# Group norm's reciprocal root by a table root and one Newton step, and the scratch half of the output projection's squares

## The chip, the cores and the metric

The kernel runs on one core of one Trainium2 chip. TensorE (PE) does the matmuls and its transposes, VectorE (DVE) the elementwise work and reductions, ScalarE (ACT) the copies and functions from a table, GpSimd (POOL) masks and some subtractions, and SyncE (SP) issues nearly all transfers. Each engine works through its own queue in order, and semaphores tie the queues together. The metric is the device time of one execution in microseconds; lower is better.

## The reference

Two layers over 512 positions of width 1024, in float32. Layer 0 mixes tokens by an RWKV-7 recurrence, layer 1 by a spatial gating unit; a gated feed-forward network follows each, and each sub-layer has a norm ahead and a norm behind it. What matters here is the end of the recurrence: its output is normalised per head of 64 values, gets a bonus term, is gated and projected, and the projection's result is normalised over its 1024 columns and added to the input.

```python
def _rmsnorm(x, g):
    x32 = x.astype(jnp.float32)
    y = x32 * lax.rsqrt(jnp.mean(x32 * x32, axis=-1, keepdims=True) + RMS_EPS)
    return (y * g.astype(jnp.float32)).astype(x.dtype)
...
    mu = jnp.mean(y, axis=-1, keepdims=True)
    var = jnp.mean(jnp.square(y - mu), axis=-1, keepdims=True)
    y = (y - mu) * lax.rsqrt(var + GN_EPS)
    y = y * gn_w.reshape(H, N).astype(f32) + gn_b.reshape(H, N).astype(f32)
    y = y + jnp.sum(r_h * k_h * r_k.astype(f32), axis=-1, keepdims=True) * v_h
    y = y.reshape(B, T, D).astype(x.dtype)
    return (y * g) @ w_o
...
        x = x + _rmsnorm(h, norm_gains[i, 1])
```

## The kernel before, in words

Nothing is kept back between stages but on-chip tiles and a few scratch tensors in memory. The 512 positions are four blocks (`tt`) of 128 partitions; the 1024 columns are two halves of 512 or eight groups of 128. Float32 products are made of three matmuls each (`mm3`, line 201) from a high and a low part, which `split` (line 178) makes with one copy on ACT and one subtraction on DVE; `weight` (line 182) loads a weight and splits it.

The recurrence treats the 16 heads in four groups `b` of four. For each group the list `PLAN` (line 35) names the parts in order: P (projections), E (`early`, line 754, with the functions Tanh, Exp and Ln on ACT), X and V (the values' projection), F (`front`, line 838), B (`back`, line 887), S (`scan`, line 985) and N (`finish`, line 1091). `front` builds the chunk matrices; ACT copies them out of the accumulators (the BX copies of lines 873, 883 and 884 among them) and POOL masks them. `back` inverts a triangular matrix: a stream transpose (line 896), a long substitution on DVE (lines 910 and 912), transposes (915 and 916), then small matmuls whose results DVE and ACT copy to `bdT` (lines 949, 959 and 968), and the products `mp` (line 973) and `gh` (line 980), which DVE adds into MV (lines 982 and 983). `scan` steps through eight chunks with the state `su` (lines 1011 and 1014) and copies its output Y out (line 1024).

N is the group norm (line 1031) with what follows it. In `group_norm` DVE sums Y (line 1038) and subtracts the mean (1040), ACT squares (1042), DVE sums the squares into `va` (1044), `rsqrt` (line 209) makes the reciprocal root, and DVE scales Y by it (1046). `rsqrt` works on DVE alone: a scaled sum (line 214), a first guess by an integer shift and subtraction (216 and 218), and three Newton steps of three instructions (221 to 223). It is called on 16 values per partition for the groups 0 to 2 and, for group 3, twice on 8 values: halves of the positions, the first when the scan is half done (line 1130). The text calls these five norms N0, N1, N2 and the first and second half of N3. `rsqrt` is also called four times on one value in the gating unit (line 1205).

`gated` (line 1076) then transposes Y on PE (`yt`, 1084), adds weight and bonus on DVE (1085), makes the gate by matmuls (`gate`, 1087 and 1088) and multiplies (1089). `yt` and `gate` share one accumulator bank, tag `pf`. For groups 0 to 2 the result goes through memory, for group 3 it stays in `OB`.

`out_proj` (line 273) is the output projection, called four times: after the recurrence, after the gating unit and after each feed-forward network. Only the first call passes `spare`. It accumulates eight banks, four blocks by two halves; with `spare` the last weight unit of both halves is held to the end (line 281) and the loop of line 335 finishes block by block. Per block and half, `post0` (line 304) and `post1` (line 314) square the accumulator on ACT with a row sum (`sumsq`, line 235, writing the squares to a scratch tile), DVE multiplies by the gain (lines 309 and 317), and `part` (line 240) and `rsqrt1` (line 248) make the row's reciprocal root: the table root on ACT (254), then reciprocal and one Newton step on DVE (256 to 258). Line 320 adds the result to `x`. The scratch tile `hn` has 1024 columns: `post1` puts its squares into the first half (`lo`) and line 317 writes the second (`hi`). Line 312 is a root on one column whose result nobody reads; it stands at the first block with `spare`, else at the last.

A table set must be on ACT before a function of it can run; where another set is there, the program holds an `ACT_TABLE_LOAD` ahead of the instruction. The order of every queue is laid down before the run by a planner that simulates the program's time (line 1289), starting from the order of the code; it threads instructions of different parts into one another.

Of the kernel before, what the change touches and what calls it, by code (L numbers as in the profile page):

```python
# [7 lines left out]
F32 = mybir.dt.float32  # L8
F32R = mybir.dt.float32r
I32 = mybir.dt.int32  # L10
AF = mybir.ActivationFunctionType
ALU = mybir.AluOpType

P = 128
# [3 lines left out]
TT = T // P  # L18
# [6 lines left out]
GN_EPS = 64e-5  # L25
# [105 lines left out]
class Trunk:  # L131
# [77 lines left out]
    def rsqrt(self, ss, n, scale, eps):  # L209
# [13 lines left out]
            v.scalar_tensor_tensor(y, t, 1.5, y, op0=ALU.add, op1=ALU.mult)  # L223
        return y

    def bcast_row(self, row):

        t = self.gp.tile([P, D], F32, name="gain", tag="gain", bufs=2)
        self.nc.gpsimd.dma_start(out=t, in_=row.partition_broadcast(P))
        return t  # L230
# [42 lines left out]
    def out_proj(self, acts, wrows, nk, row, xts, store=None, tail=3, norm=None, spare=None, mid=None, after=()):  # L273


        nc = self.nc
        v = nc.vector
        gain = self.bcast_row(row)
        nu = nk // 2
        cols = [slice(0, 512), slice(512, 1024)]  # L280
        late = (1, 1) if spare else (0, tail)
        accs, f0, part = [None, None], [], []

        def mms(half, k, tt, w):
            tok = slice(tt * P, (tt + 1) * P)
            hi, lo = acts(k)
            self.mm3(accs[half][tt], (hi[:, tok], lo[:, tok]), w, k == 0, k == nk - 1)

        def unit(half, u):
            own = spare if half and u < nu - late[1] else None  # L290
            with ExitStack() as order:
                for ins in after:
                    order.enter_context(self.tc.issue_after(ins.ins))
                hi, lo = self.weight(wrows(u)[:, :, cols[half]], spare=own)
            return [(2 * u + j, (hi[:, j, :], lo[:, j, :])) for j in range(2)]

        def first(half):
            accs[half] = self.accs(half)
            for u in range(nu - late[half]):
                for k, w in unit(half, u):  # L300
                    for tt in range(TT):
                        mms(half, k, tt, w)

        def post0(tt, junk):
            acc = accs[0][tt]
            s = self.sumsq(acc, junk)
            if tt % 2 == 0:
                f0.append(self.f0p.tile([P, 2, 512], F32, name="f0", tag="f0", bufs=2))
            v.tensor_tensor(f0[-1][:, tt % 2, :], acc, gain[:, cols[0]], op=ALU.mult)
            part.append(self.part(s, 1.0 / D, RMS_EPS))  # L310
            if tt == (0 if spare else TT - 1):
                nc.scalar.activation(junk[:, 0:1], part[tt][0], AF.Sqrt)

        def post1(tt, hn):
            acc, lo, hi = accs[1][tt], hn[:, 0:512], hn[:, 512:1024]
            s = self.sumsq(acc, lo)
            v.tensor_tensor(hi, acc, gain[:, cols[1]], op=ALU.mult)
            y = self.rsqrt1(s, part[tt], 1.0 / D)
            for f, c in ((f0[tt // 2][:, tt % 2, :], cols[0]), (hi, cols[1])):
                v.scalar_tensor_tensor(xts[tt][:, c], f, y[:, 0:1], xts[tt][:, c], op0=ALU.mult, op1=ALU.add)  # L320
                if store is not None and tt == TT - 1:
                    nc.sync.dma_start(out=store[tt * P:(tt + 1) * P, c], in_=xts[tt][:, c])
            if store is not None and tt < TT - 1:
                nc.sync.dma_start(out=store[tt * P:(tt + 1) * P, :], in_=xts[tt])

        hn_tile = lambda: self.sm.tile([P, D], F32, name="hn", tag="hn", bufs=2)
        first(0)
        if not spare:
            for tt in range(TT):
                post0(tt, hn_tile()[:, 0:512])  # L330
        if mid:
            mid()
        first(1)
        ends = [[kw for u in range(nu - late[half], nu) for kw in unit(half, u)] for half in range(2)]
        for tt in range(TT):
            for half in range(2):
                for k, w in ends[half]:
                    mms(half, k, tt, w)
            if norm and tt >= LAG:
                norm.step(tt - LAG, xts[tt - LAG])  # L340
            hn = hn_tile()
            if spare:
                post0(tt, hn[:, 512:1024])
            post1(tt, hn)
        if norm:
            for tt in range(TT - LAG, TT):
                norm.step(tt, xts[tt])
            norm.finish()
# [181 lines left out]
    def rwkv(self, x0):  # L530
        nc, i, tc = self.nc, self.i, self.tc
        v, a, g = nc.vector, nc.scalar, nc.gpsimd
        mm = nc.tensor.matmul
        with ExitStack() as ctx:
# [14 lines left out]
            def e2(name, shape=(P, 2, T), dt=F32):  # L549
                return rp.tile(list(shape), dt, name=name, tag="e2", bufs=E2)  # L550
# [41 lines left out]
            for tt in range(TT):  # L592
                hn = e2("hn", (P, D))
# [437 lines left out]
            def group_norm(Y, tts):  # L1031

                n, n4 = len(tts), 4 * len(tts)
                ts = slice(tts[0], tts[-1] + 1)
                y4 = Y[:, ts].rearrange("p t q (h v) -> p (t q h) v", h=2)
                yf = Y[:, ts].rearrange("p t q f -> p (t q f)")
                mu = self.sm.tile([P, n4], F32, name="mu", tag="mu", bufs=2)
                v.tensor_reduce(mu, y4, axis=mybir.AxisListType.X, op=ALU.add)
                v.tensor_scalar(mu, mu, 1.0 / 64, None, op0=ALU.mult)
                v.tensor_tensor(y4, y4, mu.unsqueeze(2).broadcast_to([P, n4, C]), op=ALU.subtract)  # L1040
                sq = self.sm.tile([P, n4, C], F32, name="hn", tag="hn", bufs=2)
                a.activation(sq.rearrange("p q v -> p (q v)"), yf, AF.Square)
                va = self.sm.tile([P, n4], F32, name="va", tag="va", bufs=2)
                v.tensor_reduce(va, sq, axis=mybir.AxisListType.X, op=ALU.add)
                rs = self.rsqrt(va, n4, 1.0 / 64, GN_EPS)
                v.tensor_tensor(y4, y4, rs.unsqueeze(2).broadcast_to([P, n4, C]), op=ALU.mult)

            def bonus(b, o):
# [42 lines left out]
            def finish(b, o, Y):  # L1091

                tts = (0, 1, 2, 3)
                group_norm(Y, tts)
                w = gate_weights(b)
                for q, ob in enumerate(bonus(b, o)):
                    gated(b, Y, q, ob, w, tts)
                    nc.sync.dma_start(out=od[2 * b + q], in_=ob)
# [3 lines left out]
            def finish_half(b, o, Y, tts):  # L1102
                group_norm(Y, tts)
                for q, ob in enumerate(OB):
                    gated(b, Y, q, ob, GW[0], tts)
# [187 lines left out]
```

## Time and profile before

| what | value |
|---|---|
| median of 3 runs | 1354.4 us (1348.42 to 1357.36) |
| the profiled execution | 1345.89 us |
| its span, first to last instruction | 1344.2 us |
| its mean granted TensorE clock | 0.979 |
| instructions | 24525 |
| group norms | 278 to 437 us of the span |
| first output projection's block loop | about 441 to 470 us |

In the profile's rows a group of instructions has its line, engine, operation, output and inputs, shapes and count, then busy time and the mean in nanoseconds of one, then the idle time just before them and what ended it. In the timeline the columns are start, duration, engine, line, operation, operands, count, and in brackets the idle time before it with the releaser. In the table of stretches each has its length, busy time of PE, weight loads, DVE, ACT and POOL with counts, granted clock, DMA share and GB/s.

### The profile page before, as it was taken

The page shows a single profiled execution, that of the slowest core. Times are in us where ns is not written, and L with a number is a line of the kernel's source. Part 1 is how long each engine was busy: PE and PEld are TensorE (multiplying, and loading weights), DVE is VectorE, ACT ScalarE, POOL GpSimd, SP SyncE. Part 2 cuts the span into 40 slices and gives each one's busy share as a digit, 9 for nine tenths or more (in the row PEclk, how much of TensorE's full clock was granted, in tenths as well). Part 3 has the DMA queues.
Part 4 walks back from the last instruction along what each step waited for, and adds up shares of the span by engine and source line. Part 5 has one row for each costly group of instructions (what it writes and reads, how often), then busy time and mean ns, then how long its engine had stood idle before and what let it go on. Part 6 is the DMA issues. An engine that isn't in the chain of part 4 may idle for free.

```text
span 1344.2 us, 24525 instructions
## 1 busy us (share of the span) xinstructions
PE 1279.7 (95%) x9812; PEld 1115.3 (83%) x9812; DVE 898.5 (67%) x1520; ACT 694.9 (52%) x1240; POOL 166.3 (12%) x306
## 2 busy tenths in 40 slices
PE   5999999988989799999999999999999999999997
PEld 3677799887767698899998887878888999998886
DVE  7975846667856589778775325575689878785223
ACT  7976884757443554445454314543464455464221
POOL 0000373665000121000000002020002000000000
PEclk9999999989889999999999999999999999999999
DMA  5146683412143233333323332343430443323231
GB/s 159 47 107 169 165 199 127 123 47 78 45 139 106 72 91 101 107 114 108 106 87 110 94 112 91 93 140 98 142 95 2 125 126 95 97 78 125 94 94 63
DMA packets 217266, 140.10 MB, mean 104 GB/s; under 512 B 67856, under 2 KB 193344, under 8 KB 217152
## 3 DMA queue, kind: packets, MB, share of 16 engines
q1 hardware_dynamic: 215856, 133.81, 34.6%
q0 software_dynamic: 1296, 4.72, 1.0%
q8 instruction: 77, 1.26, 0.4%
q14 instruction: 37, 0.30, 0.1%
HBM read 124.35 MB, written 14.16 MB: 103 GB/s over the span
## 4 chain that ended last, share of the span: by engine, by line
PE 58%; DVE 5%; ACT 1%; issue 1%; DMA 0%; SPq 0%; DVEq 0%; ACTq 0%
PE acc L204 24%; PE Q L204 11%; PE Z L204 7%; PE R L204 7%; PE gu L204 5%; PE u L204 3%; DVE wlo L180 1%; DVE wsum L387 1%; PE s L1227 1%; PE ptr L267 0%; ACT whi L179 0%; DVE braw L106 0%; DVE hT L62 0%; DVE bc L180 0%; DVE x L320 0%
## 5 line engine op out<-in xcount | busy, mean ns | idle before, releaser
L180 DVE TENSOR_TENSOR wlo<-wraw,whi 128x1024 fp32r<-128x1024 f32 x109 | 133.6, 1226 | 197.8 <-ACT whi L179 197.4
L179 ACT CAST whi<-wraw 128x1024 fp32r<-128x1024 f32 x109 | 114.2, 1048 | 224.1 <-PE acc L204 140.9
L204 PE MATMUL acc<-whi,actw 128*128 128x512 f32 x704 | 220.7, 394 | 0.0
L204 PE MATMUL Q<-bc,whi 128*128 128x256 f32 x864 | 157.2, 282 | 3.5 <-ACT hn L431 2.2
L204 PEld LDWEIGHTS acc<-whi,actw 128*128 128x128 f32 x704 | 132.3, 188 | 30.7
L204 PE MATMUL acc<-wlo,actw 128*128 128x512 f32 x352 | 138.7, 394 | 0.0
L204 PEld LDWEIGHTS Q<-bc,whi 128*128 128x128 f32 x864 | 133.8, 190 | 4.3 <-ACT hn L431 2.6
L179 ACT CAST whi<-wsum 128x1024 fp32r<-128x1024 f32 x72 | 75.2, 1050 | 90.3 <-PE Q L204 31.3
L204 PE MATMUL Q<-bc,wlo 128*128 128x256 f32 x432 | 121.7, 282 | 0.0
L204 PE MATMUL Z<-bc,whi 128*128 128x256 f32 x576 | 106.8, 283 | 0.0
L204 PE MATMUL R<-bc,whi 128*128 128x256 f32 x576 | 105.3, 281 | 0.8 <-ACT whi L179 0.8
L180 DVE TENSOR_TENSOR wlo<-wsum,whi 128x1024 fp32r<-128x1024 f32 x72 | 87.0, 1220 | 20.3 <-ACT whi L179 19.1
L204 PE MATMUL gu<-hT,whi 128*128 128x256 f32 (+1 forms) x384 | 91.5, 331 | 5.0 <-DVE hT L62 3.6
L179 ACT CAST whi<-wq 128x1024 fp32r<-128x1024 f32 x54 | 56.6, 1049 | 66.0 <-PE R L204 22.3
L204 PEld LDWEIGHTS R<-bc,whi 128*128 128x128 f32 x576 | 88.9, 188 | 1.3 <-ACT whi L179 1.0
L204 PEld LDWEIGHTS Z<-bc,whi 128*128 128x128 f32 x576 | 89.7, 190 | 0.1
L180 DVE TENSOR_TENSOR wlo<-wq,whi 128x1024 fp32r<-128x1024 f32 x54 | 67.4, 1250 | 28.8 <-ACT whi L179 28.7
L204 PE MATMUL Z<-bc,wlo 128*128 128x256 f32 x288 | 81.4, 283 | 2.3 <-DVE wlo L180 2.3
L204 PE MATMUL proj<-xsp,whi 128*128 128x512 f32 x256 | 82.4, 401 | 1.3 <-ACT r L674 1.3
L204 PEld LDWEIGHTS Q<-bc,wlo 128*128 128x128 f32 x432 | 82.1, 190 | 0.0
L204 PE MATMUL R<-bc,wlo 128*128 128x256 f32 x288 | 81.0, 281 | 0.0
L204 PEld LDWEIGHTS acc<-wlo,actw 128*128 128x128 f32 x352 | 66.0, 188 | 15.3
(346 smaller groups left out, 2841.2 us busy)
## 6 DMA issues: line engine op xcount, KB each, us to landing
wraw<-in_ffn_w_down_dram SPq DMA_DIRECT2D x44, 512.0 KB, 3.7
wq<-in_ffn_w_gate_dram SPq DMA_DIRECT2D x72, 256.0 KB
wq<-in_ffn_w_up_dram SPq DMA_DIRECT2D x72, 256.0 KB, 4.2
wraw<-in_rwkv_w_rkv_dram SPq DMA_DIRECT2D x24, 512.0 KB, 5.4
wraw<-in_sgu_w_in_dram SPq DMA_DIRECT2D x16, 512.0 KB, 4.5
x<-in_x_dram SPq DMA_DIRECT2D x8, 512.0 KB, 3.4
ST<-sb SPq DMA_DIRECT2D x8, 512.0 KB
MV<-sa SPq DMA_DIRECT2D x32, 128.0 KB, 3.5
```

What stands on the lines that cost most here:

```text
L179: self.nc.scalar.copy(hi, src)
L180: self.nc.vector.tensor_tensor(lo, src, hi.bitcast(F32), op=ALU.subtract)
L204: self.nc.tensor.matmul(out, l, r, start=start, stop=stop, skip_group_check=resumed)
L387: v.tensor_tensor(s, x, y, op=ALU.add)
L1227: mm(acc[:, tt * P:(tt + 1) * P], vt[tt][:, m * P:(m + 1) * P], wsT[:, m, :], start=True, stop=True)
```

## The change

The group norm calls a new `rsqrtn`: the scaled sum on DVE, the root on ACT, the reciprocal on DVE and one Newton step of three instructions on DVE. `rsqrt` stays for the gating unit. In the output projection with `spare`, line 312's root is no longer issued, and `post0` writes its squares to the first half of `hn` instead of the second.

```diff
+    def rsqrtn(self, ss, n, scale, eps):
+
+        sm, v = self.sm, self.nc.vector
+        c, r, m = (sm.tile([P, n], F32, name=t, tag=t) for t in ("nr_a", "nr_y", "nr_t"))
+        v.tensor_scalar(c, ss, scale, eps, op0=ALU.mult, op1=ALU.add)
+        self.nc.scalar.activation(r, c, AF.Sqrt)
+        v.reciprocal(r, r)
+        v.tensor_tensor(m, r, r, op=ALU.mult)
+        v.scalar_tensor_tensor(m, m, -0.5, c, op0=ALU.mult, op1=ALU.mult)
+        v.scalar_tensor_tensor(r, m, 1.5, r, op0=ALU.add, op1=ALU.mult)
+        return r
...
-            if tt == (0 if spare else TT - 1):
+            if not spare and tt == TT - 1:
                 nc.scalar.activation(junk[:, 0:1], part[tt][0], AF.Sqrt)
...
             if spare:
-                post0(tt, hn[:, 512:1024])
+                post0(tt, hn[:, 0:512])
...
-                rs = self.rsqrt(va, n4, 1.0 / 64, GN_EPS)
+                rs = self.rsqrtn(va, n4, 1.0 / 64, GN_EPS)
```

## The prediction

> **What bounds the kernel now.** First the page's busy times, then the stretches of 10 us around the five group norms and the tail of the output projection.
>
> ```profile
> span 1344.2 us, 24525 instructions
> PE 1279.7 (95%) x9812; PEld 1115.3 (83%) x9812; DVE 898.5 (67%) x1520; ACT 694.9 (52%) x1240; POOL 166.3 (12%) x306
> 280.00:290.00 10.00, 8.12 (x108) 7.38 (x107) 7.12 (x16) 8.93 (x21) 6.07 (x12) 0.84 0.30 83
> 330.00:340.00 10.00, 6.71 (x136) 5.79 (x138) 9.74 (x32) 5.04 (x8) 3.13 (x7) 0.57 0.13 45
> 400.00:410.00 10.00, 10.00 (x90) 8.36 (x90) 7.38 (x24) 3.16 (x9) 0.00 (x0) 1.00 0.50 157
> 430.00:440.00 10.00, 10.00 (x47) 8.16 (x46) 6.12 (x19) 2.57 (x4) 0.00 (x0) 1.00 0.37 106
> 440.00:450.00 10.00, 8.56 (x40) 6.79 (x38) 4.52 (x10) 5.50 (x13) 0.00 (x0) 1.00 0.18 53
> 450.00:460.00 10.00, 9.28 (x40) 7.62 (x41) 8.23 (x28) 3.24 (x12) 0.00 (x0) 0.83 0.20 54
> ```
>
> In the stretches the columns are length, then busy time of PE, PEld, DVE, ACT and POOL, then granted clock, DMA share and GB/s. TensorE is busy 95% of the span, so the change can gain only where PE stands still or runs at a lowered clock, and where a released wait ends there. All it touches lies between 287 us (first group norm) and 464 us (last output-projection matmul). The later stages keep their instructions and should shift as a block. The five norms meet different limits: at N0 (280 to 290) ACT is the fullest engine, at N1 (330 to 340) DVE is, at N2 (400 to 410) and at the second half of N3 (430 to 440) PE is at 10.00 of 10. In the tail PE has a hole and then the clock of 0.83.
>
> **Part 1: the root itself.** Per norm the old form issues 12 DVE instructions (lines 214 to 223), the new one 5 on DVE and one on ACT.
>
> ```profile
> L222 DVE SCALAR_TENSOR_TENSOR nr_t<-nr_t,nr_a 128x16 f32<-128x16 f32 x9 | 1.7, 186 | 0.1
> L214 DVE TENSOR_SCALAR nr_a<-va 128x16 f32<-128x16 f32 x3 | 0.7, 241 | 0.0
> L254 ACT ACTIVATE rr<-ss,rc 128x1 f32<-128x1 f32 x4 | 1.3, 318 | 0.3 <-DVE rh L245 0.3
> L256 DVE RECIPROCAL rr<-rr 128x1 f32<-128x1 f32 x3 | 0.5, 158 | 0.0
> L312 ACT ACT_TABLE_LOAD x1 | 1.3, 1283 | 0.9 <-DVE rh L245 0.9
> L803 ACT ACT_TABLE_LOAD x3: 1283/1283/1283, 110.2 to 175.6; - x3
> ```
>
> Seven DVE instructions of about 0.18 us go away net: 1.3 us of DVE busy time per norm, 6.3 us in all. A square root of 16 values is not in the trace; the nearest row, one value with pointer bias, takes 0.32 us, so I take 0.3. The reciprocal of 16 values lies between 0.16 (one value) and 16 times that, 2.5; since the other operations hardly differ between 1 and 16 values I take 0.2, and the upper end would add 2.3 us to each chain that PE waits for (N1 and the first half of N3, 4.6 us in all). The last table before N0 was loaded at 175.6 us for line 803's exponential, so N0's root must load another, 1.28 us of ACT; from there on ACT does copies, squares and scalings, which reload nothing in the trace, until the tail.
>
> What this is worth, norm by norm:
>
> ```profile
> 287.25 0.38 DVE L214 TENSOR_SCALAR nr_a<-va 128x16 f32<-128x16 f32 x1
> 288.24 0.37 ACT L883 COPY BX<-bkt 64x256 f32<-64x256 f32 x1 [0.16 <-PE bkt L879]
> 290.37 1.22 DVE L1046 TENSOR_TENSOR Y<-Y,nr_y 128x1024 f32<-128x1024 f32 x1
> ```
>
> N0. The input of the root is there at 287.63. ACT is taken until 288.08 (0.16 idle before 288.24), then come 1.28 of table and 0.3 of root: 289.7. Four DVE instructions of 0.2 follow, so line 1046 starts at about 290.5 against 290.37: +0.1. Queued behind the waiting reciprocal on DVE are line 1046, the stream transpose of line 896 and line 982, whose MV the scan's matmuls wait for. On ACT the four BX copies from 288.24 on move back by up to 1.6 us. Ends: -0.6 where the planner fills the wait with line 896, +1.6 where PE waits for those copies in full. I take +0.2, because DVE, which orders line 982, hardly moves.
>
> ```profile
> 340.04 0.17 DVE L222 SCALAR_TENSOR_TENSOR nr_t<-nr_t,nr_a 128x16 f32<-128x16 f32 x1
> 340.15 0.29 DVE L910 TENSOR_TENSOR tm<-LX,Dm 128x126 f32<-128x126 f32 x1
> 343.92 0.69 DVE L968 COPY bdT<-T2p 32x512 f32<-32x512 f32 x1
> 344.66 2.08 PE L973 MATMUL mp<-MVt,bdT 128*128 128x128 f32 x8 [1.86 <-DVE bdT L968]
> ```
>
> N1. The old root is threaded into the substitution of lines 910 and 912, and the next instruction starts 0.11 us after a 0.17 us one, so seven fewer are worth about 0.12 each: 0.85 us. This DVE queue ends in line 968, for which PE stood 1.86 us, so I count -0.85. Ends: 0, where the queue waits for ACT instead, and -1.4, seven at 0.2.
>
> N2 counts 0, hidden by PE's 10.00 of 10; without that cover it would be worth N1's 0.85.
>
> ```profile
> 423.52 0.69 DVE L1046 TENSOR_TENSOR Y<-Y,nr_y 128x512 f32<-128x512 f32 x1
> 424.56 0.44 PE L1084 MATMUL yt<-ident,Y 128*128 128x128 f32 x2 [0.29 <-DVE su L1011]
> 436.00 0.69 DVE L1046 TENSOR_TENSOR Y<-Y,nr_y 128x512 f32<-128x512 f32 x1
> 443.51 0.38 PE L1084 MATMUL yt<-ident,Y 128*128 128x128 f32 x2
> ```
>
> N3, first half: Y is ready at 424.21 and transposed at 424.56, so here PE follows DVE; seven instructions less one trip to ACT, -0.5 (ends 0 and -1.4). Second half: Y is ready at 436.69, its transposes stand in PE's order at 443.51, 6.8 us later, behind matmuls that run without a gap: 0. Should the planner move these transposes forward, that is a rival below.
>
> **Part 2: the tail without the priming root.** Line 312 with its load goes away for this projection alone, since the norm's root has already loaded the table.
>
> ```profile
> 445.09 0.60 ACT L237 ACTIVATE hn<-acc 128x512 f32<-128x512 f32 x1 [1.68 <-PE acc L204]
> 445.58 0.19 ACT L237 ACTIVATION_READ_ACCUMULATOR hn<-acc 128x1 f32 x1
> 446.64 1.28 ACT L312 ACT_TABLE_LOAD   x1 [0.86 <-DVE rh L245]
> 447.93 0.20 ACT L312 ACTIVATE hn<-rc 128x1 f32<-128x1 f32 x1
> 448.04 0.58 ACT L237 ACTIVATE hn<-acc 128x512 f32<-128x512 f32 x1
> ...
> 448.75 0.69 DVE L317 TENSOR_TENSOR hn<-acc,gain 128x512 f32<-128x512 f32 x1 [2.12 <-ACT hn L237]
> ...
> 450.26 0.40 DVE L1089 TENSOR_TENSOR ob<-gate,ob 128x256 f32<-128x256 f32 x1
> ...
> 450.72 0.64 PE L1084 MATMUL yt<-ident,Y 128*128 128x128 f32 x2 [2.16 <-DVE ob L1089]
> ```
>
> Read as a chain: ACT stands from 445.77 to 448.04 (0.86 waiting for line 245, 1.28 load, 0.20 root); the second square comes 2.3 us late, if its accumulator was done; line 317 waits 2.12 us for it on DVE; behind line 317 in that queue stands line 1089; and PE, through with the gate at 448.56, waits 2.16 us for line 1089 before it can reuse the gate's bank. Without line 312 the second square waits for PE alone: in the dense stretch from 430 on 47 matmuls took 10 us, 0.21 us each, and the second accumulator is six of them behind the first, about 446.4, so 1.6 us earlier. Line 1089 then comes up at about 448.9 and PE resumes at 449.4: -1.3. Ends: 0, where the queue ahead of line 1089 fills up otherwise, and -2.1, where the gate's end at 448.56 is all that is left.
>
> The granted clock of 0.83 in 450 to 460 stands for 1.7 us of full speed lost right behind that hole. A shorter hole may keep the clock: ends 0 and -1.7, I take -0.7. The Trainium skill, page "TensorE: Matmul & The Clock Gate", section "What's actually happening", has the clock fall after an idle window of about 3.4 us. The hole here was 2.16 us and the clock fell, so the row speaks for a lower threshold than the rule; by the rule alone this term would be nothing either way.
>
> **Part 3: the other half of hn.** The view of line 317's 16 instructions names what ended DVE's idle time before them:
>
> ```profile
>   ACT hn L237: 26.6, 9
> ```
>
> All 26.6 us of it, in 9 waits, ended with line 237's square. With the halves as they were, line 317 writes the half into which the first square wrote, but that square ended at 445.69, over 2 us before the one that released it. So the exchange counts 0; the cover is the second square's wait, and without that cover the write would be held at most by one 0.60 us square.
>
> **Sum.** N0 +0.2, N1 -0.85, N3 -0.5, tail -1.3, clock -0.7: -3.15, say -3.2 us. The profiled execution took 1345.9 us (span 1344.2 and 1.7 around it) and would take 1342.7; it lies 8.5 below the median of the runs, 1354.4, so on the median I forecast 1351.2 us.
>
> The Trainium skill, page "ScalarE: Activation LUTs", section "What ACT_TABLE_LOAD costs", speaks against the change at N0: it adds a drain of about 1.38 us to each switch. In the tail's rows the root starts 0.01 us after its load ends, and the time before the load is given to line 245, so no drain shows; were it real at N0, the sum would be -1.8.
>
> **Rivals.**
>
> A, the roots wait on ACT (slower). ACT's queue is in order. At N0 it is 8.93 of 10 busy and the load falls among the BX copies that feed PE: the full 1.6 us. At N1 and the first half of N3 the reciprocal stands on DVE behind an ACT queue that itself waits for DVE copies (lines 949 and 1014), and a net loss of 1.5 us at each (about one of the waits below) replaces the gains there: +3.0. With the tail's and the clock's -2.0 the sum is +2.6: 1357.0. The kernel is slower than before as soon as these two losses pass 0.4 us together.
>
> ```profile
> ACT bdT L949 <- DVE bdT L949: 5.4, 5, 2.2
> ACT su L1014 <- DVE su L1011: 11.4, 8, 3.8
> ```
>
> In the waits between 270 and 470 us these two took 16.8 us in 13 waits, 1.3 us each. For it: that, and ACT's fill at N0. Against it: ACT at 5.04 of 10 at N1. Chance 0.25.
>
> B, nothing arrives. PE catches the earlier DVE work with matmuls already queued, and line 1089 comes no earlier because the second projection tile's squares stand before it. Sum 0: 1354.4. For it: PE's 10.00 in two of the stretches. Chance 0.2.
>
> C, the planner (line 1289) reorders the tail. The order of each queue is laid down before the run from estimated durations, and any changed estimate can change it. If Y's transposes of the second half move up by their 6.8 us, the hole (2.16) and the low clock (1.7) both vanish, with N1's and N3's ends of 1.4 each: -6.7, or 1347.7. For it: DVE and ACT at 6.12 and 2.57 of 10 in 430 to 440. Against it: PE's matmuls there have no gap to move into. Chance 0.12.
>
> D, the change doesn't do what it says: a table other than the root's is loaded again between the norms and the tail, so the load merely moves to the line 254 root there. The tail's gain shrinks to the 0.20 us root and the clock's goes: +0.2 -0.85 -0.5 -0.2, or -1.35: 1353.0. Nothing after 175.6 us loads one before 446.64, so 0.03.
>
> **How the numbers follow.** The forecast gets 0.4. Its own range, all low ends (-7.2) to all high ends (+1.6), is 1347.2 to 1356.0; the reciprocal's 4.6 would lift the top to 1360.6. The range for the time runs from 1342 (rival C with the 6.0 us by which the lowest of the three runs lies under their median) to 1360 (rival A with the 3.0 by which the highest lies above it). A measurement of this kernel tells about 1% from no change, 13.5 us; no case reaches that, and only a reordering beyond those named could: 0.04 faster, 0.03 slower, 0.93 within.
>
> **What would show it.** Right: no load between 440 and 450 us, one at N0; the second square under 1 us behind the first accumulator; PE's wait for line 1089 under 1.2 us; the clock in the 10 us behind it above 0.9; line 968 at N1 about 0.9 earlier against line 1038. Wrong: DVE idle before the new reciprocals released by ACT for more than 1 us each, or a tail in another order of PE's transposes and gates, or stages after 470 us that change their length.

## The result, and the profile after

| | before | changed |
|---|---|---|
| median of 12 runs | 1351.62 us (1347.94 to 1357.36) | 1337.04 us (1334.05 to 1347.77) |
| profiled execution, span | 1345.89, 1344.2 us | 1335.05, 1333.4 us |
| mean granted clock there | 0.979 | 0.988 |

The ratio is 0.9899, 95% interval 0.9876 to 0.9921: 1.0% faster, 14.6 us between the medians. The forecast was 3.2 us, and the time lies below the range on record. The 1354.4 us that the forecast started from are the median of three runs; over the twelve in this table it is 1351.62. The changed kernel's profile is the execution with the highest clock of its twelve (0.976 to 0.988, mean 0.9835), so its account shows somewhat more clock than the usual run has.

The page of the changed kernel and its stretches (columns as in the prediction; its lines are 12 further on than before's from line 226 on):

```profile
span 1333.4 us, 24506 instructions
PE 1272.8 (95%) x9812; PEld 1109.0 (83%) x9812; DVE 891.1 (67%) x1485; ACT 694.5 (52%) x1244; POOL 172.5 (13%) x306
...
280.00:290.00 10.00, 7.68 (x105) 7.03 (x104) 7.66 (x13) 8.37 (x19) 5.71 (x12) 0.85 0.32 87
330.00:340.00 10.00, 7.75 (x132) 6.38 (x130) 9.74 (x26) 7.36 (x14) 2.83 (x5) 0.83 0.30 104
340.00:350.00 10.00, 9.36 (x83) 8.06 (x84) 9.59 (x30) 3.52 (x7) 0.00 (x0) 1.00 0.07 26
440.00:450.00 10.00, 8.47 (x34) 6.75 (x33) 7.96 (x25) 3.45 (x12) 0.00 (x0) 0.83 0.18 55
```

The same 9812 matmuls keep TensorE busy 6.9 us less, and outside them it stands 60.6 us instead of 64.5 (span less busy). A matmul that is the same and shorter has run at a higher clock: the lost clock, one minus the mean times the span, is 28.2 us before and 16.0 after. So the gain shows twice in the accounts, as less waiting and as clock.

Where it arises is read from one stage. It begins with the first Y copy of group 0 and ends with the last gate product of group 3. These rows are from the timelines, first before, then after:

```profile
255.63 0.37 ACT L1024 COPY Y<-Yp 128x256 f32<-128x256 f32 x1 [2.25 <-PE Yp L1022]
...
324.26 0.69 DVE L935 TENSOR_TENSOR Qs<-Qp,id 128x512 f32<-128x512 f32 x1 [0.16 <-PE Qp L932]
...
454.72 0.42 DVE L1089 TENSOR_TENSOR ob<-gate,ob 128x256 f32<-128x256 f32 x1 [0.83 <-PE gate L1088]
```

```profile
257.80 0.37 ACT L1036 COPY Y<-Yp 128x256 f32<-128x256 f32 x1 [2.25 <-PE Yp L1034]
...
290.18 1.38 DVE L1058 TENSOR_TENSOR Y<-Y,nr_y 128x1024 f32<-128x1024 f32 x1
...
316.72 0.69 DVE L947 TENSOR_TENSOR Qs<-Qp,id 128x512 f32<-128x512 f32 x1 [0.76 <-PE Qp L944]
...
445.75 0.42 DVE L1101 TENSOR_TENSOR ob<-gate,ob 128x256 f32<-128x256 f32 x1 [1.00 <-PE gate L1100]
```

The stage took 199.1 us before and 188.0 after, 11.1 less of a span that is 10.8 shorter. The largest single step lies between N0's multiplication and `Qs` of group 2's inverse: 33.9 us before (290.37 to 324.26), 26.5 after. Nothing of the root stands between them. What differs is the order. The two programs' queues agree up to N0; from there on 1194 of TensorE's 8233 matmul instructions stand in another place. In the two timelines, before and after, the first product of that inverse (`Qp`) looks like this:

```profile
312.44 2.10 DVE L915 STREAM_TRANSPOSE hn<-Dm 128x1024 f32<-128x1024 f32 x1
...
314.97 0.32 PE L932 MATMUL Qp<-hn,LA 32*32 32x32 f32 x14
...
316.01 1.16 PE L865 MATMUL lm<-MV,ST 128*128 128x128 f32 x8
...
319.42 0.45 PE L932 MATMUL Qp<-hn,LA 32*32 32x32 f32 x30
319.80 1.16 PE L865 MATMUL lm<-MV,ST 128*128 128x128 f32 x8
...
323.81 0.38 PE L932 MATMUL Qp<-hn,LA 32*32 32x32 f32 x22
```

```profile
312.92 0.89 PE L944 MATMUL Qp<-hn,LA 32*32 32x32 f32 x80
...
316.29 0.38 PE L944 MATMUL Qp<-hn,LA 32*32 32x32 f32 x20
```

Before, `Qp` is threaded between group 3's `lm` products and is drawn out over 9 us, though its operand from line 915 was complete at 314.54. After, it is through in 3.7 us. TensorE is full in both, at a granted clock of 1.00. Busy time can't tell the two apart; only the order of what it is busy with. The stretch is also shorter because other work stands behind it: it holds 354 matmul records after, 417 before.

What the whole stage gained is read from its two accounts, first before, then after, and from the stretch from 340 us on before (the one ahead of it, 330 to 340, is in the prediction; those after are shown above):

```profile
255.63:454.72 199.09, 178.15 (x2557) 149.31 (x2558) 137.16 (x336) 101.61 (x238) 48.69 (x115) 0.91 0.29 86
```

```profile
257.80:445.75 187.95, 170.04 (x2557) 142.80 (x2558) 129.66 (x296) 101.55 (x242) 48.50 (x115) 0.97 0.31 91
```

```profile
340.00:350.00 10.00, 8.14 (x97) 7.22 (x96) 9.53 (x22) 1.85 (x3) 0.00 (x0) 0.58 0.01 2
```

The same 2557 matmuls keep TensorE busy 8.1 us less, and it stands 3.0 us less outside them. So most of the 11.1 us is clock in these two executions. The largest part of it lies between 330 and 350 us: 8.5 us lost before (0.57 and 0.58), 1.7 after (0.83 and 1.00).

So two theories. P: the planner's new order brings the gain. D: VectorE's seven fewer instructions per root bring it, in any order.

### The profile page after: what moved, and what is told of

It is laid out like the page before. It is cut to its first block, busy times and chain, and to the rows that moved or that the text cites. A ratio compares the mean times of both kernels' runs of the same rounds, so it can differ in the third digit from the quotient of the medians.

```text
span 1333.4 us, 24506 instructions
## 1 busy us (share of the span) xinstructions
PE 1272.8 (95%) x9812; PEld 1109.0 (83%) x9812; DVE 891.1 (67%) x1485; ACT 694.5 (52%) x1244; POOL 172.5 (13%) x306
## 4 chain that ended last, share of the span: by engine, by line
PE 62%; DVE 9%; DMA 3%; ACT 2%; issue 2%; SPq 1%; POOL 0%; DVEq 0%; ACTq 0%
PE acc L204 27%; PE Q L204 9%; PE R L204 6%; PE Z L204 6%; PE gu L204 5%; PE u L204 3%; DVE wlo L180 2%; DMA wq<-in_ffn_w_up_dram 1%; DVE wsum L399 1%; PE gh L992 1%; DMA wraw<-in_rwkv_w_o_dram 1%; ACT whi L179 1%; PE mp L985 1%; DVE hT L62 1%; PE s L1239 1%
```

## The experiments

A version can be held in another one's order. The listed instructions of each engine are chained by edges that say only "issue after", with no semaphore:

```diff
+def hold(tc, nc):
+    info = mybir.DependencyInfo(mybir.DependencyClass.NoSync, mybir.DependencyReason.DATA)
+    for engine, text in HOLD.items():
...
+        for first, second in zip(order, order[1:]):
+            tc.add_manual_dep(second, first.name, info, reason="hold")
...
         build(tc, ins, outs[0])
+        hold(tc, nc)
```

`HOLD` lists, engine by engine, the places in the code's order. Each kernel was timed against the one before, on the same chip; the stage and the granted clock in it are from one profile each. That clock differs between executions of the same queues (0.97 in the changed kernel's first profile, 0.95 in e5), so a difference of a few us between two stages can be clock.

| run | root | order | tail | stage, us | clock in it | ratio, 95% |
|---|---|---|---|---|---|---|
| before | old | old | old | 199.1 | 0.91 | 1 |
| changed | new | new | new | 188.0 | 0.97 | 0.9899, 0.9876 to 0.9921 |
| e1 | new | old | new | 200.2 | 0.91 | 0.9955, 0.9933 to 0.9976 |
| e15 (e1 again) | new | old | new | 197.6 | 0.93 | 0.9971, 0.9954 to 0.9989 |
| e2 | old | new | old | 194.7 | 0.93 | 0.9962, 0.9939 to 0.9985 |
| e3 | new | free | old | 188.1 | 0.95 | 0.9945, 0.9921 to 0.9969 |
| e4 | old | free | new | 198.4 | 0.92 | 0.9994, 0.9967 to 1.0022 |
| e5 (the change again) | new | new | new | 187.9 | 0.95 | 0.9896, 0.9865 to 0.9926 |
| e6 | old | first part new | old | 193.6 | 0.94 | 0.9950, 0.9930 to 0.9969 |
| e7 | old | second part new | old | 199.0 | 0.93 | 1.0007, 0.9985 to 1.0029 |
| e8 | new | new | old | 188.1 | 0.95 | 0.9904, 0.9875 to 0.9932 |
| e9 | new, padded | new | new | 195.0 | 0.93 | 0.9946, 0.9921 to 0.9970 |
| e10 | new in N2, N3 second half | new | new | 191.9 | 0.97 | 0.9929, 0.9903 to 0.9954 |
| e11 | new in N0, N1, N3 first half | new | new | 188.8 | 0.95 | 0.9942, 0.9921 to 0.9963 |
| e12 | new | 15 moved | new | 197.0 | 0.90 | 0.9950, 0.9926 to 0.9974 |
| e13 | new | 6 more moved | new | 189.4 | 0.93 | 0.9911, 0.9890 to 0.9932 |
| e14 | new | more again | new | 197.1 | 0.90 | 0.9948, 0.9927 to 0.9969 |

### Order and root taken apart: e1, e2

> The changed kernel, whole, but every engine's queue is held in the order of the kernel before by order-only edges (no semaphore); the root's square roots stand in ScalarE's queue where the planner puts them. Theory P (the planner's new order brings the gain): 1349 to 1353 us against some 1351.6 of before, ratio 0.998 to 1.001, and b=2's Qs (line 947) starts 33 to 35 us behind N0's line 1058, as before (33.9), where after had 26.5. Theory D (fewer DVE instructions bring the gain in any order): 1337 to 1341 us, ratio 0.989 to 0.992.

> The kernel before, with its twelve-instruction root, its priming root and its upper half, but every engine's queue held in the order that the changed kernel has (the root's twelve instructions stand where the five stand). Theory P: 1337 to 1342 us, ratio 0.989 to 0.993, Qs of b=2 26 to 28 us behind N0's line 1046. Theory D: 1348 to 1353 us, ratio 0.997 to 1.001.

Neither theory had it. Each half alone brings some 0.4%, together they bring 1.0%. In the stages of these profiles, clock included, the order alone is worth 4.4 us (199.1 to 194.7), and the root on top of it 6.7 (to 188.0). `Qs` of e2 stood 25.7 us behind N0's multiplication, where the new order puts it. In the old order e1 shows no gain in the stage, but a low clock shortly behind N0, which a second profile of the same kernel lacks (first e1, then e15):

```profile
290.00:300.00 10.00, 10.00 (x59) 9.19 (x59) 6.09 (x14) 4.85 (x11) 7.42 (x18) 0.62 0.12 28
```

```profile
290.00:300.00 10.00, 10.00 (x87) 8.86 (x88) 9.13 (x28) 3.88 (x9) 7.38 (x18) 1.00 0.26 60
```

> The changed kernel in the old order once more. Its stage was 200.1 us in the first profile, against 199.1 before, with a clock of 0.62 between 290 and 300 us that no other profile has. If that fall belongs to this version: 199 to 201 us again. If it was this execution's own: 194 to 197 us, that is five times up to 1.3 us less where VectorE bounds. By the times: ratio 0.994 to 0.997 again.

The low clock was that execution's own; without it the stage is 197.6, a little above what I gave. The timeline of e15 shows what the 1.5 us gained are:

```profile
255.47 0.37 ACT L1036 COPY Y<-Yp 128x256 f32<-128x256 f32 x1 [2.25 <-PE Yp L1034]
...
435.87 0.69 DVE L1058 TENSOR_TENSOR Y<-Y,nr_y 128x512 f32<-128x512 f32 x1
...
449.96 0.44 PE L1096 MATMUL yt<-ident,Y 128*128 128x128 f32 x2 [1.17 <-DVE ob L1101]
...
453.04 0.42 DVE L1101 TENSOR_TENSOR ob<-gate,ob 128x256 f32<-128x256 f32 x1
```

The last multiplication by the root comes 180.4 us after the first Y copy, as before (255.63 to 436.00). In this order the five new roots show nothing in the stage by then. The operand of group 3's `Qp` was begun 2.1 us earlier than before (88.1 against 90.2 us from the first Y copy), and `Qs` came 0.3 earlier. Between them, in e15:

```profile
343.54 2.09 DVE L927 STREAM_TRANSPOSE hn<-Dm 128x1024 f32<-128x1024 f32 x1
...
364.17 1.29 PE L944 MATMUL Qp<-hn,LA 32*32 32x32 f32 x128
```

The operand is there at 345.63 and waits 18.5 us for `Qp`'s turn in TensorE's queue; the gain is given back there. Part of that may be clock: by rows of 2 us TensorE ran at one half until 351.4 here, 95.9 us from the first Y copy, and before until 348.4, which is 92.8 us from it. These rows can't separate the place in the queue from the lower clock. The 1.5 us come later, in the tail.

### Which edit, which part of the order: e3 to e8

> Only the new root; priming root and upper half stay as before; the planner is free. Its queues agree with the changed kernel's up to the tail of the output projection. Theory P, with the order up to the tail as what counts: 1337 to 1342 us, ratio 0.989 to 0.993; N0 to the last line 1101 as in after. Were the tail's two edits the cause: 1349 to 1352.

> Only the tail's two edits (no priming root, lower half); the old root; the planner is free, and leaves the queues of TensorE and SP as they were. Theory P: 1350 to 1352.5 us, ratio 0.999 to 1.001. My sum on record for the tail: -1.3 us and -0.7 by the clock, so 1349.6, ratio 0.9985.

The root alone makes the planner choose the new order up to the tail, the tail's edits alone leave TensorE's as it was. E4's interval holds both theory P's 1 and my 0.9985. It doesn't try the tail as the sum has it, either: with the old root the group norms load no table, and the load moves to the first row root of the tail, as rival D has it:

```profile
448.18 1.28 ACT L266 ACT_TABLE_LOAD   x1
```

E3 has the stage of the changed kernel, 188.1, but loses 4.8 us later: from the last product into `gu`, the bank of the second feed-forward network's first products, to the end it took 314.9 us (1026.1 to 1341.0), the changed kernel 310.1 (1023.3 to 1333.4). With the priming root in the program the planner had laid the queues from the tail on in a third order: 533 of TensorE's instructions stand elsewhere than in the changed kernel's.

> The new root alone, with the priming root and the upper half as before, held in the changed kernel's order throughout (with a free planner the later FFNs had another order, and the profile lost some 4 us there after 1033 us). If that other order was the loss: as the changed kernel, ratio 0.990 to 0.992. If the tail's two edits bring something of their own in the new order: ratio 0.993 to 0.995.

Held in the changed kernel's order throughout, the same edit gives 0.9904, and those last 310 us are 310.0. The tail's two edits bring nothing of their own in this order that these intervals could show.

> The changed kernel once more, beside the others of this call. The sum of what the two halves of the change brought by themselves (new root in the old order -4.8 us of mean, old root in the new order -5.7) gives about 1341, ratio 0.992; if they help each other, 1337, ratio 0.990 as at first. Of the gain, about half should stand in the clock (mean granted clock 0.983 against 0.978: 7 us of the span) and about 6 us in the rest.

The change repeats its ratio, nearer the second figure than the sum of the halves, as do the first result and e8. The intervals reach to the sum's 0.992, so that the halves help each other is likely and not shown.

> The kernel before, its queues held in the new order from N0 to b=2's block inverse and its products (TensorE's queue up to place 2300), and in the old order from there on. If the inverse of b=2 ahead of front(3)'s matmuls is what the order brings: 1344 to 1347 us, ratio 0.995 to 0.998, and Qs of b=2 27 us behind N0's line 1046. If it is the later part: 1349 to 1352, ratio 0.999 to 1.001.

> The complement: old order up to b=2's products, new order from there on (N2, N3, the output projection and the FFN's start). If the first part is what the order brings: 1349 to 1352 us, ratio 0.999 to 1.001. If the later part: 1344 to 1347, ratio 0.995 to 0.998.

The first part of the order carries all of its gain, the second none; the second holds the tail. The low clock behind that part goes with it. First e6, then e7:

```profile
325.00:355.00 30.00, 26.27 (x417) 22.11 (x413) 28.39 (x70) 14.72 (x30) 6.61 (x15) 0.89 0.17 53
```

```profile
325.00:355.00 30.00, 24.17 (x448) 20.49 (x448) 27.09 (x65) 12.97 (x27) 6.50 (x15) 0.72 0.13 41
```

In these 30 us the clock is 0.66 to 0.77 in all five profiles with the old first part (before, e1, e15, e4, e7) and 0.83 to 0.94 in all twelve with the new one, whatever the root. So the order brings a part of its gain as clock; which of its moves does that isn't shown. Not every move in the first part was tried alone, so that it is `Qp`'s place, and not another move beside it, is read from the rows and not shown by itself.

### What a root is worth in the new order: e9, e10, e11

```diff
+                pad = self.sm.tile([P, 16], F32, name="nr_h", tag="nr_h")
+                for _ in range(7):
+                    v.tensor_tensor(pad[:, 0:n4], va, va, op=ALU.mult)
```

> The changed kernel in its own order, with seven small VectorE products of 16 (or 8) values behind each group norm's last multiplication (their result is not used): VectorE issues as many instructions as with the old root, but the norm itself is ready as early as with the new one. Theory O (VectorE's queue is the bound of this stage, each instruction taken out of it counts wherever it stands): the stage from the first Y copy to the last line with the gate product is 194 to 195 us as with the old root in this order (194.7), ratio 0.995 to 0.997. Theory L (the norm's own delay counts): 188 to 190 us, ratio 0.989 to 0.992.

In e9's trace the padding is

```profile
L1061 DVE TENSOR_TENSOR nr_h<-va x35: 151/174/372, 291.8 to 436.1; 128x16 f32<-128x16 f32 x21, 128x8 f32<-128x8 f32 x14
```

35 instructions of 0.174 us are 6.1 us. The stage grew by 7.0, to 195.0, although nothing waits for them and each norm needs no more than with the new root. The ratio, 0.9946, is just below O's 0.995 to 0.997, and its interval (from 0.9921) just clears L's 0.989 to 0.992. So L fails: instructions that no norm waits for cost about their time, at the five places where they were put. That VectorE's queue carries the stage, as O has it, fits and isn't shown by this alone: the clock in the stage was 0.93 here and 0.95 to 0.97 in the changed kernel, so a part of the 7.0 us is clock.

> The changed kernel's order and tail, with the new root only in N2 and in N3's second half, the two that the sum on record counts as nothing since TensorE is full there; the old root in the other three. Sum on record: stage as with the old root everywhere, 194.7 us, ratio 0.996. Theory O: two times 1.3 us less, 192.0, ratio 0.993 to 0.995.

> The complement: the new root in N0, N1 and N3's first half, the old one in N2 and N3's second half, same order. Sum on record (+0.2, -0.85 and -0.5): 193.5 us. Theory O: three times 1.3 us less, 190.8, ratio 0.991 to 0.993.

E10's stage lies on O's figure (191.9 for 192.0), 2.8 us under e2's. But its clock there was 0.97 and e2's 0.93, the ratios 0.9929 and 0.9962 have intervals that overlap, and over the runs e10's time without the lost clock is 2.1 us under before's, e2's 1.9. So that the two norms counted as nothing are worth anything but clock isn't shown. E11's stage is 2.0 below O's figure, while its ratio is 0.001 above O's range; without the lost clock its runs are 5.6 us under before's. The two stage gains, 2.8 and 5.9, are more than the 6.7 of all five, so a single norm's share isn't known to better than some 2 us.

### An order that should be better: e12, e13, e14

In the changed kernel ScalarE and VectorE stand in front of a split of projection weights that waits for its transfer, with copies of group 3's inverse behind it:

```profile
377.49 1.04 ACT L179 CAST whi<-wraw 128x1024 fp32r<-128x1024 f32 x1 [4.23 <-DMA wraw<-in_rwkv_w_o_dram]
378.55 0.57 ACT L980 COPY bdT<-T2p 32x512 f32<-32x512 f32 x1
...
378.56 1.23 DVE L180 TENSOR_TENSOR wlo<-wraw,whi 128x1024 fp32r<-128x1024 f32 x1 [5.19 <-ACT whi L179]
```

> The changed kernel with 15 instructions moved in its queues between 368 and 385 us, nothing else: on ScalarE and VectorE the copies of b=3's inverse and of the scan go ahead of two splits of the output projection's weights that wait there for their transfer (4.2 and 5.2 us of idle time), and on TensorE the product of b=3's inverse, the scan's and the first merging product go ahead of the projection's matmuls on those weights. If the queue's order is what bounds here, the inverse of b=3 is ready 3 to 6 us earlier, and the stage is 183 to 186 us instead of 188, 1333 to 1335 us, ratio 0.986 to 0.988. If TensorE's work from 390 us on bounds (full there): as the changed kernel, 188, ratio 0.990.

The page of e12, a row of its timeline, and stretches of 2 us:

```profile
span 1342.1 us, 24504 instructions
...
PE 1283.5 (96%) x9812; PEld 1117.8 (83%) x9812; DVE 891.8 (66%) x1485; ACT 695.4 (52%) x1244; POOL 172.6 (13%) x306
```

```profile
387.93 1.26 PE L992 MATMUL gh<-BX,MVt 64*128 64x128 f32 x12 [1.91 <-ACT MVt L987]
```

```profile
388.00:390.00 2.00, 2.00 (x17) 1.78 (x18) 2.00 (x4) 0.15 (x1) 0.00 (x0) 0.83 0.11 18
390.00:392.00 2.00, 2.00 (x12) 1.77 (x13) 2.00 (x5) 0.15 (x1) 0.00 (x0) 0.50 0.98 328
...
404.00:406.00 2.00, 2.00 (x18) 1.55 (x15) 0.91 (x3) 0.71 (x2) 0.00 (x0) 0.50 0.00 0
406.00:408.00 2.00, 2.00 (x20) 1.76 (x18) 0.83 (x4) 1.02 (x4) 0.00 (x0) 0.90 0.07 16
```

TensorE stands less, 58.6 us outside its matmuls (span less busy) against 60.6, and yet the stage is 9 us longer, and the clock takes it: one wait of 1.91 us, and the clock stands at one half for 17.1 us (0.68 us in the first of these stretches, 14 between, 2 and 0.4 in the last two), with TensorE busy all the while: 8.5 us lost.

> The version with 15 moved instructions, and six more moves: on ScalarE the first merged copy (line 987) and a Y copy go ahead of the split that waited 2.69 us for its transfer at 386.2 us, on VectorE the sum for mu and the first two additions to MV go ahead of that split's second half, and b=3's copy goes ahead of a scan product. TensorE's wait of 1.91 us at 387.9, behind which the clock stood at 0.5 for 17 us, should be gone. If that one hole made the version slow: clock loss between 380 and 410 us at most 2 us, stage 184 to 188 us, 1332 to 1336 us, ratio 0.985 to 0.988. If the clock falls in this stretch whatever hole is there: stage 190 to 197, ratio 0.991 to 0.996.

With that hole closed the clock holds from 384 on and the ratio is 0.9911, about the changed kernel's, no better. The gain that is left is taken elsewhere. In e13 and in the changed kernel TensorE waits near 367 (2.87 and 2.26 us); behind it the clock is low for

```profile
368.00:370.00 2.00, 0.86 (x45) 0.86 (x46) 0.30 (x1) 0.40 (x2) 0.00 (x0) 0.68 0.54 141
370.00:372.00 2.00, 2.00 (x59) 1.94 (x55) 1.12 (x3) 1.27 (x3) 0.00 (x0) 0.50 0.36 134
...
380.00:382.00 2.00, 2.00 (x7) 1.50 (x5) 0.00 (x0) 1.79 (x4) 0.00 (x0) 0.50 0.07 16
382.00:384.00 2.00, 2.00 (x24) 1.47 (x23) 1.43 (x2) 0.46 (x3) 0.00 (x0) 0.90 0.07 16
```

13.7 us in e13, and in the changed kernel's profile for

```profile
368.00:370.00 2.00, 2.00 (x92) 1.94 (x89) 1.06 (x2) 0.99 (x2) 0.00 (x0) 0.71 0.78 229
370.00:372.00 2.00, 2.00 (x15) 1.69 (x12) 1.29 (x3) 1.04 (x2) 0.41 (x2) 0.50 0.15 55
372.00:374.00 2.00, 2.00 (x21) 1.22 (x21) 1.23 (x1) 1.20 (x4) 0.00 (x0) 0.93 0.19 41
```

3.4 us. Another execution of the same kernel gave another length: in e5 the wait there was 2.02 us, and the low clock behind it lasted 6.8 us.

> As the run before, and the first merging product (line 985) goes ahead of five of the projection's matmuls, the first products of line 992 ahead of the scan's Yp, with the copies that belong to them. The inverse's chain of b=3 is then some 3 us shorter again. If queue order bounds here and the clock holds: stage 182 to 186, ratio 0.984 to 0.987; if the clock falls again: 188 to 197, ratio 0.990 to 0.996.

The clock fell again, here behind a wait of 2.49 us at 392 as well, for 6.8 us. No version beat the changed kernel. Over the runs, with the lost clock as above:

| kernel, runs | mean, us | mean clock | lost clock | rest |
|---|---|---|---|---|
| before, 23 (beside e13) | 1349.5 | 0.9787 | 28.8 | 1320.7 |
| changed, first 12 | 1337.8 | 0.9835 | 22.1 | 1315.8 |
| e5 (the change again), 6 | 1337.2 | 0.9822 | 23.8 | 1313.4 |
| e12, 7 | 1345.4 | 0.9750 | 33.6 | 1311.8 |
| e13, 6 | 1337.4 | 0.9812 | 25.2 | 1312.2 |
| e14, 12 | 1342.8 | 0.9770 | 30.8 | 1311.9 |

The moves took 1 to 2 us out of e5's rest and 4 out of the first runs', and the clock took as much or more. By the scatter of the runs, figures in the last two columns are known to between 0.5 and 2 us.

## Why the prediction was wrong, point by point

**The step that failed** is the sum itself: every term was costed in the order of the kernel before. That a changed estimate can reorder the queues stood in rival C, but only for the tail, worth 6.7 us at a chance of 0.12. C's mechanism, a reordering, was right, its place wrong. The order that counts lies between N0 and group 2's inverse and its products (e6 0.9950), while the part that holds the tail brings nothing (e7 1.0007). And in that new order the root, which the sum had at 1.15 us, takes the ratio from 0.9962 (e2) to 0.9904 (e8). The chance of 0.04 for faster hung on "a reordering beyond those named", and that is what came.

**Part 1, the durations.** The table root took 0.215 us in the median (0.3 taken), the reciprocal of 16 values 0.25 (0.2 taken), the load 1.28. The root's line in the changed kernel, and N0's rows from its timeline:

```profile
L231 ACT ACTIVATE nr_y<-nr_a x5: 208/215/216, 288.9 to 423.6; 128x16 f32<-128x16 f32 x3, 128x8 f32<-128x8 f32 x2
...
  DVE nr_y L232: 0.6, 2
```

```profile
286.65 1.28 ACT L231 ACT_TABLE_LOAD   x1
288.92 0.22 ACT L231 ACTIVATE nr_y<-nr_a 128x16 f32<-128x16 f32 x1 [0.99 <-DVE nr_a L230]
...
288.72 0.17 DVE L230 TENSOR_SCALAR nr_a<-va 128x16 f32<-128x16 f32 x1
289.17 0.25 DVE L232 RECIPROCAL nr_y<-nr_y 128x16 f32<-128x16 f32 x1 [0.28 <-ACT nr_y L231]
```

The load stands ahead of the root and runs while the root's input is still being made. So from line 230 to the multiplication it takes 1.46 us where the old root took 3.12 (287.25 to 290.37): 1.7 us less, where the prediction worked out +0.1 and took +0.2.

**N1 -0.85, N3 first half -0.5, N2 and N3's second half 0.** In the old order all five together show 0.0 us up to the last multiplication (e15). The sign named for N1, its `bdT` copy 0.9 us earlier against the sum for `mu`, did not appear there: 17.57 us from 324.02 to 341.59, against 17.65 before. So -0.85 took VectorE's queue for the bound, while group 3's `Qp` behind it still had to wait for its turn. In the new order all five are worth about 6.7 in the stage, clock included, and some 2.8 of that at most belong to the two zeros (e10). Whether "hidden by PE's 10.00 of 10" was a wrong reading therefore stays open; it did rest on the order of TensorE's queue, and that order changed.

**The tail, -1.3 and -0.7 by the clock.** About right in the order for which it was worked out: in e15 PE's wait for line 1101 is 1.17 us (2.16 before, under 1.2 foretold) and the last 18.7 us of the stage became 17.2, though the second square came 1.9 us behind the first (445.33 and 447.26), not the 1.3 of six matmuls. The granted clock behind the wait is

```profile
450.00:460.00 10.00, 10.00 (x50) 8.19 (x51) 7.28 (x23) 3.88 (x11) 0.51 (x1) 1.00 0.18 54
```

where it was 0.83. That the shorter wait kept the clock isn't shown: in e4 it held at 1.00 behind a wait of 1.90 us. In the new order the wait is 0.79 us with the priming root (e8) and without it, since N0's root has brought the table already; the clock in 440 to 450 was 0.83 in the changed kernel's profile and 1.00 in e8's.

**The exchange of halves, 0.** No run tries it alone. E8 against e5 holds it and the priming root together: 0.9904 and 0.9896, nothing that their intervals could show.

**Rival A** is refuted: VectorE waited for the new roots on ScalarE 0.6 us in all, in two waits (the last row of the root's line above). **B** fails with the time. **D** didn't occur: the tail has no load.

**The clock** entered the sum at one place with -0.7. Over the runs its change is 5 us of 12 (28.8 to 23.8 in the table above). By the same account, each against the runs of before beside it, the order alone took 3.9 us out of the lost clock and 1.9 out of the rest (e2), the root with the tail's edits about 3 and 1 to 2 (e1, e15), and order and root together 5.4 and 7 (e5) or 7.4 and 4 (e8). So each half alone gained mostly clock, and about half of the whole gain is clock.

## What to carry to other kernels

Where a planner lays the queues, first put the new and the old order side by side: an edit that saves a microsecond can set off a reordering worth several, and its sign can't be read from the edit. To cost an edit, hold the order and change the edit, then hold the edit and change the order; one stage's length in a profile tells such halves apart better than the whole time, if the clock granted in it is read beside it. And whether an edit off the full engine counts hangs on the order of that engine's queue: the same roots brought 1.5 us of the stage in the old order (e15) and 6.6 in the new (e2 to e8), clock included.

## What the runs showed of the hardware

How long a fallen clock lasts was not what I expected. Waits of 2.26 us in the changed kernel, 2.87 in e13 and 1.91 in e12 were followed by one half of the clock for 3.4, 13.7 and 17.1 us: one, four and five times 3.4. The same place of the same queue gave 6.8 us in e5, two steps. The Trainium skill, page "TensorE: Matmul & The Clock Gate", section "What's actually happening", has a free-running window of about 3.4 us, with the clock back after one busy window. The step of 3.4 agrees. That one busy window brings it back doesn't: TensorE was 2.00 of 2 busy in e12 from 388 to 406 and stayed at one half. What decides the number of steps stays open. The kind of matmul alone doesn't: e5 has the matmuls of the changed kernel, and in e13 projection matmuls of 512 columns ran from 372.65 on while the clock stayed at one half.
